# One weight tile in three of the last matrix product: its lower part by an accumulating DMA

## The chip, the cores and the metric

One core of one Trainium2 chip. The time is device time of one execution in microseconds (us), and lower is better.

## The reference

A decoder layer on x, 256 tokens by 2048 channels, in float32:

```python
h = rms_norm(x, norm1_g); z = h @ w_in                     # 2048 -> 13312
# ... three branches (pooling, Conformer convolution, gated short convolution), merged by sigmoid gates ...
x = x + merged @ w_o
h = rms_norm(x, norm2_g)
up = causal_dwconv(h @ ffn_up, ffn_conv_w)                 # 2048 -> 2 x 5504
gt, vl = jnp.split(up, 2, axis=-1)
x = x + (jax.nn.silu(gt) * vl) @ ffn_down                  # 5504 -> 2048: the product that is changed
out = rms_norm(x, final_g)
```

## The kernel before, in words

Every matrix product is made of three products of float32r operands. A weight tile w, loaded as float32 into `raw`, is split into an upper part `wh`, which is w rounded to float32r, and a lower part `wl` = w - wh. The activations are split in the same way and lie in one tile, upper part in the first 256 columns and lower part in the next 256. TensorE adds up act_high x wh, act_low x wh and act_high x wl in float32 in PSUM.

`load_w` (L67) makes one weight tile. SyncE (SP) issues the load of 128 x 1024 numbers, 512 KB, into a `raw` buffer (L64); ScalarE (ACT) copies it to `wh`, which rounds (L75); VectorE (DVE) subtracts `wh` from `raw` into `wl` (L76). There are five `raw` buffers and three each of `wh` and `wl` (L59, L72, L73). A tile's `wh` can be written when TensorE has made the last product with the `wh` that lay in the buffer before it; `wl` likewise; and the next load into a `raw` buffer can be issued when ACT and DVE have read it.

The last product, with `ffn_down`, is `gemm_n` (L128), called four times, once for each 512 output columns (L606 to L610). K is 5504, in 43 blocks of 128 rows; a weight tile holds two blocks (kt=2), so that one call has 22 tiles, the last of them a half. For each tile `products` issues eight matmuls with `wh` (L143 and L145 by turns) and then four with `wl` (L150), each of 512 columns. The first two tiles of the first call are made ahead, before the last posts of the stage before (L572). What follows a call (residual, squares, the norm's gain: `take`, L582) is a post; it is issued after the second tile of the next call (L158). The fourth call (L610) has its last eight blocks in a large buffer of their own and ends with `finish`.

The order of the instructions on each engine is fixed when the program is built, by a scheduler: it takes the instructions by priority (the order in which the code issues them) as their inputs and buffers come free by its own reckoning. On the chip each engine runs its queue in that order and waits at each instruction for the semaphores of what it depends on. GpSimd (POOL) has no DMA and no work in the calls of the last product but for one small power per half at the end (L598).

Of the kernel before, what the change touches and what calls it, by code (L numbers as in the profile page):

```python
# [12 lines left out]
F32 = mybir.dt.float32  # L13
F32R = mybir.dt.float32r
AF = mybir.ActivationFunctionType
ALU = mybir.AluOpType
PSUM = bass.MemoryType.PSUM

P = 128
# [6 lines left out]
KF = FF // P  # L26
# [17 lines left out]
def hybrid_block(ctx: ExitStack, tc, xT, x, vec, w_in, w_gate, gate_b, pool_w, pool_p, conf_p, sconv_p, w_o, up, down, fg, out):  # L44


    nc = tc.nc

    const = ctx.enter_context(tc.tile_pool(name="const", bufs=1))
    wp = ctx.enter_context(tc.tile_pool(name="wp", bufs=3))  # L50
# [7 lines left out]
    def load_raw(src):  # L58
        raw = wp.tile([P, 1024], F32, name="raw", bufs=5)  # L59
        n = math.prod(src.shape[1:])  # L60
        v = raw[:, 0:n]
        if len(src.shape) == 3:
            v = v.rearrange("p (a b) -> p a b", a=src.shape[1])
        held["load"] = nc.sync.dma_start(v, src).ins  # L64
        return v, n

    def load_w(src, dst=None):  # L67

        raw, n = load_raw(src)
        kt = src.shape[1]  # L70
        if dst is None:
            wh = wp.tile([P, 1024], F32R, name="wh")  # L72
            wl = wp.tile([P, 1024], F32R, name="wl")  # L73
            dst = [w[:, 0:n].rearrange("p (a b) -> p a b", a=kt) for w in (wh, wl)]
        nc.scalar.copy(dst[0], raw)  # L75
        held["split"] = nc.vector.tensor_sub(dst[1], raw, dst[0].bitcast(F32)).ins  # L76
        return dst

    posts = deque()
# [3 lines left out]
    def run_posts():  # L86
        while posts:
            posts.popleft()()
# [4 lines left out]
    def tick(n):  # L93

        due[0] += n
        while due[0] >= 1 and background:
            due[0] -= 1
            with tc.issue_after(held["split"]):
                background.popleft()()
        if not background:  # L100
            due[0] = 0
# [23 lines left out]
    def first_weights(src, n=2):  # L125
        return [load_w(src[:, 2 * i:2 * i + 2, :]) for i in range(n)]

    def gemm_n(src, act, nk, kt=2, ahead=(), ticks=0, last=None, finish=None):  # L128

        if last is None:
            ps = psg.tile([P, 2, 512], F32, name="g")
            out = [ps[:, t, :] for t in range(2)]
        else:
            out = [psm.tile([P, 512], F32, name="m") for t in range(2)]

        def products(ts, k0, wh, wl):
            n = wh.shape[1]
            for kk in range(n):  # L140
                k = k0 + kk
                for t in ts:
                    nc.tensor.matmul(out[t], lhsT=act[:, k, t * P:(t + 1) * P], rhs=wh[:, kk, :],  # L143
                                     start=(k == 0), stop=False)
                    nc.tensor.matmul(out[t], lhsT=act[:, k, S + t * P:S + (t + 1) * P], rhs=wh[:, kk, :],  # L145
                                     start=False, stop=False)
            for kk in range(n):
                k = k0 + kk
                for t in ts:
                    nc.tensor.matmul(out[t], lhsT=act[:, k, t * P:(t + 1) * P], rhs=wl[:, kk, :],  # L150
                                     start=False, stop=(k == nk - 1))

        nb = nk - (8 if last is not None else 0)
        for i, k0 in enumerate(range(0, nb, kt)):
            n = min(kt, nb - k0)
            products((0, 1), k0, *(ahead[i] if i < len(ahead) else load_w(src[:, k0:k0 + n, :])))
            tick(ticks)
            if i == 1:  # L158
                run_posts()
        if last is not None:  # L160
            chunks = [(k0, load_w(src[:, k0:k0 + 2, :], [last[:, o + k0 - nb:o + k0 - nb + 2, :] for o in (0, 8)]))
                      for k0 in range(nb, nk, 2)]
            for t in range(2):
                for k0, w in chunks:
                    products((t,), k0, *w)
                finish(t, out[t])
        return out
# [315 lines left out]
    def branch(b, n, proj, act, ticks=0, ahead=()):  # L483
        posts.append(gate(b, n, gemm_n(w_gate[4 * b + n], hT, KD, ticks=ticks, ahead=ahead)))
        posts.append(add_branch(b, n, gemm_n(proj[n], act, KW, ticks=ticks)))

    ahead = first_weights(w_gate[0])
# [3 lines left out]
    for n in range(4):  # L491
        branch(0, n, pool_p, bA, 2, ahead)
        ahead = ()
# [7 lines left out]
    ahead = first_weights(w_o[0])  # L501
# [9 lines left out]
    def residual(ps, xs, ss):  # L511

        nc.vector.tensor_add(xs, ps, xs)
        nc.scalar.activation(scratch, xs, AF.Square, accum_out=ss)
# [28 lines left out]
    for n in range(4):  # L543
        posts.append(norm_chunk(n, gemm_n(w_o[n], merged, KD, ahead=ahead)))
        ahead = ()
# [4 lines left out]
    fa = fpool.tile([P, KF, 2 * S], F32R, name="fa")  # L550
    background.extend([*pause(1), second_mean_squares, second_rstd])
    with tc.tile_pool(name="up", bufs=2) as upp:
# [19 lines left out]
        ahead = first_weights(down[0])  # L572
# [9 lines left out]
    def take(n, ps):  # L582
        def go():
            for t in range(2):
                residual(ps[t], x1[:, t, 512 * n:512 * n + 512], ss3[:, t, n:n + 1])
            xs = x1[:, :, 512 * n:512 * n + 512]
            nc.vector.tensor_mul(xs, xs, fgb[:, 512 * n:512 * n + 512].unsqueeze(1).broadcast_to([P, 2, 512]))
            if n == 2:
                nc.vector.reduce_sum(part, ss3[:, :, 0:3], axis=mybir.AxisListType.X)
                nc.vector.tensor_scalar(part, part, 1.0 / D, EPS, op0=ALU.mult, op1=ALU.add)  # L590
        return go

    def finish(t, ps):

        r = const.tile([P, 1], F32, name=f"r3{t}")
        residual(ps, x1[:, t, 1536:D], ss3[:, t, 3:4])
        nc.vector.tensor_scalar(r, ss3[:, t, 3:4], 1.0 / D, part[:, t:t + 1], op0=ALU.mult, op1=ALU.add)
        nc.gpsimd.tensor_tensor(r, r, neg_half[:, 0:1], op=ALU.pow)  # L598
        nc.scalar.activation(x1[:, t, 0:768], x1[:, t, 0:768], AF.Copy, scale=r)
        nc.scalar.dma_start(ov[:, t, 0:768], x1[:, t, 0:768])  # L600
        nc.vector.tensor_scalar_mul(x1[:, t, 768:1536], x1[:, t, 768:1536], r)
        nc.sync.dma_start(ov[:, t, 768:1536], x1[:, t, 768:1536])
        nc.vector.scalar_tensor_tensor(x1[:, t, 1536:D], x1[:, t, 1536:D], r, fgb[:, 1536:D], op0=ALU.mult, op1=ALU.mult)
        nc.sync.dma_start(ov[:, t, 1536:D], x1[:, t, 1536:D])

    for n in range(3):  # L606
        posts.append(take(n, gemm_n(down[n], fa, KF, ahead=ahead)))
        ahead = ()
    room = hp.tile([P, 16, 512], F32R, name="hT")
    gemm_n(down[3], fa, KF, last=room, finish=finish)  # L610
# [48 lines left out]
```

## Time and profile before

| | |
|---|---|
| median of 2 runs | 1500.69 us (1499.91 to 1501.47) |
| the profiled execution's own time | 1499.96 us |
| its span, first to last instruction | 1498.2 us |
| TensorE (PE) busy | 1480.2 us, 99% |
| DVE busy | 1051.6 us, 70% |
| ACT busy | 733.3 us, 49% |
| POOL busy | 22.8 us, 2% |
| mean granted TensorE clock | 0.998 of full speed |

The span runs from the first instruction to the last; the execution's own time has some 1.8 us around it. Busy shares are means over the whole program. The calls of the last product begin at about 1255.8 us of the span and their products end at about 1489.9 us.

### The profile page before, as it was taken

To read this page: it belongs to the slowest core of one execution; us is meant where nothing else is said; L and a number is where in the kernel's file an instruction comes from. 1 tells how busy PE (TensorE), PEld (TensorE's weight loads), DVE (VectorE), ACT (ScalarE), POOL (GpSimd) and SP (SyncE) were. 2 spreads that over 40 slices of the span, in tenths; PEclk is the share of its full clock that TensorE was granted. 3 is DMA by queue.
4 is the path that set the end of the run, shared out by engine and by line. 5 is a ranking of instruction groups with operands and counts; after the bars stand their busy time and mean duration, and the time that the engine had idled before them with its cause. 6 is when DMAs were issued, how large, how long until landed. Compare 5 with 4: busy or idle time off the path is not lost.

```text
span 1498.2 us, 19991 instructions
## 1 busy us (share of the span) xinstructions
PE 1480.2 (99%) x7546; PEld 1263.8 (84%) x7546; DVE 1051.6 (70%) x1402; ACT 733.3 (49%) x935; POOL 22.8 (2%) x87
## 2 busy tenths in 40 slices
PE   7999999999999999999999999999999999999997
PEld 6888888888888888888888888888888888888886
DVE  5868888888888775555557777777777777455453
ACT  6554454444444454444555555555555555344343
POOL 0000000000001100000000000000000000000000
PEclk9999999999999999999999999999999999999999
DMA  8755555676666666667655555555555556666663
GB/s 274 241 190 189 176 190 185 183 233 202 198 207 198 199 201 197 193 193 239 185 184 188 188 188 190 188 189 189 189 189 187 191 186 217 192 199 194 188 199 120
DMA packets 83169, 293.13 MB, mean 196 GB/s; under 512 B 9344, under 2 KB 9856, under 8 KB 82688
## 3 DMA queue, kind: packets, MB, share of 16 engines
q1 hardware_dynamic: 82640, 291.06, 61.3%
q8 instruction: 59, 0.97, 0.2%
q10 hardware_dynamic: 432, 0.79, 0.1%
q14 instruction: 38, 0.31, 0.1%
HBM read 289.72 MB, written 2.10 MB: 195 GB/s over the span
## 4 chain that ended last, share of the span: by engine, by line
PE 97%; DMA 2%; issue 0%; DVE 0%; ACT 0%; DVEq 0%; POOLq 0%; POOL 0%; SPq 0%; ACTq 0%
PE g L114 32%; PE g L118 17%; PE g L143 15%; PE g L145 15%; PE g L150 15%; DMA raw<-in_w_in 1%; PE m L150 1%; PE m L143 1%; PE m L145 1%; DMA raw<-in_xT 0%; PE m L478 0%; PE m L527 0%; ACT wh L75 0%; DVE wl L76 0%; DMA g<-in_vec 0%
## 5 line engine op out<-in xcount | busy, mean ns | idle before, releaser
L76 DVE TENSOR_TENSOR wl<-raw,wh 128x1024 fp32r<-128x1024 f32 (+1 forms) x537 | 650.1, 1212 | 372.0 <-ACT wh L75 365.9
L75 ACT CAST wh<-raw 128x1024 fp32r<-128x1024 f32 (+1 forms) x537 | 556.4, 1036 | 651.3 <-PE g L145 265.5
L114 PE MATMUL g<-hT,wh 128*128 128x512 f32 x2144 | 539.9, 393 | 9.7 <-ACT wh L75 5.3
L114 PEld LDWEIGHTS g<-hT,wh 128*128 128x128 f32 x2144 | 385.5, 189 | 80.0 <-ACT wh L75 11.4
L118 PEld LDWEIGHTS g<-hT,wl 128*128 128x128 f32 x2144 | 293.7, 191 | 21.7
L118 PE MATMUL g<-hT,wl 128*128 128x256 f32 x2144 | 300.1, 282 | 0.0
L143 PE MATMUL g<-wh,hT 128*128 128x512 f32 x384 | 150.1, 391 | 0.0
L145 PE MATMUL g<-wh,hT 128*128 128x512 f32 x384 | 149.5, 389 | 0.0
L284 DVE SCALAR_TENSOR_TENSOR confwork<-confwork,vecs 128x256 f32<-128x256 f32 x240 | 106.3, 478 | 0.0
L150 PE MATMUL g<-wl,hT 128*128 128x512 f32 x384 | 102.7, 389 | 0.0
L145 PE MATMUL g<-wh,fa 128*128 128x512 f32 x258 | 100.4, 389 | 0.0
L143 PE MATMUL g<-wh,fa 128*128 128x512 f32 x258 | 100.4, 389 | 0.0
L150 PEld LDWEIGHTS g<-wl,hT 128*128 128x128 f32 x384 | 72.1, 188 | 15.0
L145 PEld LDWEIGHTS g<-wh,hT 128*128 128x128 f32 x384 | 72.1, 188 | 14.8
L143 PEld LDWEIGHTS g<-wh,hT 128*128 128x128 f32 x384 | 72.1, 188 | 14.8
L563 DVE SCALAR_TENSOR_TENSOR cv<-sp,vecs,cv 128x256 f32<-128x256 f32 x172 | 71.7, 479 | 0.0
L150 PE MATMUL g<-wl,fa 128*128 128x512 f32 x258 | 69.2, 389 | 0.0
L150 PEld LDWEIGHTS g<-wl,fa 128*128 128x128 f32 x258 | 48.4, 188 | 10.1
L143 PEld LDWEIGHTS g<-wh,fa 128*128 128x128 f32 x258 | 48.4, 188 | 10.0
L145 PEld LDWEIGHTS g<-wh,fa 128*128 128x128 f32 x258 | 48.4, 188 | 10.0
L143 PE MATMUL g<-wh,merged 128*128 128x512 f32 x128 | 50.1, 391 | 0.0
L145 PE MATMUL g<-wh,merged 128*128 128x512 f32 x128 | 49.8, 389 | 0.0
(145 smaller groups left out, 1079.5 us busy)
## 6 DMA issues: line engine op xcount, KB each, us to landing
raw<-in_up SPq DMA_DIRECT2D x172, 512.0 KB, 4.6
raw<-in_w_gate SPq DMA_DIRECT2D x96, 512.0 KB, 4.4
raw<-in_w_in SPq DMA_DIRECT2D x92, 512.0 KB, 4.3
raw<-in_down SPq DMA_DIRECT2D x84, 512.0 KB, 4.2
raw<-in_w_o SPq DMA_DIRECT2D x32, 512.0 KB, 3.6
raw<-in_pool_p SPq DMA_DIRECT2D x16, 512.0 KB, 5.0
raw<-in_sconv_p SPq DMA_DIRECT2D x16, 512.0 KB, 4.7
raw<-in_conf_p SPq DMA_DIRECT2D x16, 512.0 KB, 4.5
```

Source lines behind the costliest of these rows:

```text
L75: nc.scalar.copy(dst[0], raw)
L76: held["split"] = nc.vector.tensor_sub(dst[1], raw, dst[0].bitcast(F32)).ins
L114: nc.tensor.matmul(ps[:, j, :], lhsT=wh[:, kk, j * P:(j + 1) * P], rhs=act[:, k0 + kk, :], start=(k0 + kk == 0), stop=False)
L118: nc.tensor.matmul(ps[:, j, 0:S], lhsT=wl[:, kk, j * P:(j + 1) * P], rhs=act[:, k0 + kk, 0:S], start=False, stop=(k0 + kk == nk - 1))
L143: nc.tensor.matmul(out[t], lhsT=act[:, k, t * P:(t + 1) * P], rhs=wh[:, kk, :], start=(k == 0), stop=False)
L145: nc.tensor.matmul(out[t], lhsT=act[:, k, S + t * P:S + (t + 1) * P], rhs=wh[:, kk, :], start=False, stop=False)
L150: nc.tensor.matmul(out[t], lhsT=act[:, k, t * P:(t + 1) * P], rhs=wl[:, kk, :], start=False, stop=(k == nk - 1))
L284: nc.vector.scalar_tensor_tensor(acc[:, c, :], src, w, acc[:, c, :], op0=ALU.mult, op1=ALU.add)
L563: nc.vector.scalar_tensor_tensor(cv[:, h, :], sp[:, h, q:q + S], V("ffn_w", c + q), cv[:, h, :], op0=ALU.mult, op1=ALU.add)
```

## The change

A second loader, `load_w_dma`, and a flag `by_dma` of `gemm_n`. In the first three calls of the last product the tiles with i % 3 == 2 (i = 2, 5, 8, 11, 14, 17, 20, seven in each call) are made by it. ACT writes `wh` as before, then a second time over the same size: `wl` = -wh. Then POOL issues a DMA from `raw` to `wl` that adds what it brings to what lies there, so that `wl` = w - wh. DVE has no part in these tiles. All other tiles, and the fourth call, are as before.

```diff
+    def load_w_dma(src):
+        raw, n = load_raw(src)
+        wh, wl = (wp.tile([P, 1024], F32R, name=w)[:, 0:n].rearrange("p (a b) -> p a b", a=src.shape[1]) for w in ("wh", "wl"))
+        nc.scalar.copy(wh, raw)
+        nc.scalar.activation(wl, wh.bitcast(F32), AF.Copy, scale=-1.0)
+        nc.gpsimd.dma_start(wl, raw, accum_op=ALU.add)
+        return wh, wl
...
-    def gemm_n(src, act, nk, kt=2, ahead=(), ticks=0, last=None, finish=None):
+    def gemm_n(src, act, nk, kt=2, ahead=(), ticks=0, last=None, finish=None, by_dma=False):
...
-            products((0, 1), k0, *(ahead[i] if i < len(ahead) else load_w(src[:, k0:k0 + n, :])))
+            load = load_w_dma if by_dma and i % 3 == 2 else load_w
+            products((0, 1), k0, *(ahead[i] if i < len(ahead) else load(src[:, k0:k0 + n, :])))
...
-        posts.append(take(n, gemm_n(down[n], fa, KF, ahead=ahead)))
+        posts.append(take(n, gemm_n(down[n], fa, KF, ahead=ahead, by_dma=True)))
```

## Rows read from the trace of the kernel before

**Rows 1.** The page's part 4, the chain of work that ended last, by engine.
```profile
PE 97%; DMA 2%; issue 0%; DVE 0%; ACT 0%; DVEq 0%; POOLq 0%; POOL 0%; SPq 0%; ACTq 0%
```

**Rows 2.** Waits of TensorE in the whole span: total us, times, longest us.
```profile
PE g L114 <- ACT wh L75: 5.3, 8, 1.0
PE g L114 <- DVE hT L254: 4.4, 1, 4.4
```

**Rows 3.** Busy time by stretch, two calls of the last product: columns in the first line.
```profile
core 0: us, PE busy (x) PEld busy (x) DVE busy (x) ACT busy (x) POOL busy (x), PEclk, DMA share, GB/s
...
1316.00:1375.00 59.00, 59.00 (x262) 48.87 (x261) 29.13 (x26) 24.64 (x27) 0.00 (x0) 1.00 0.66 194
1375.00:1434.00 59.00, 59.00 (x262) 48.83 (x262) 29.13 (x27) 24.64 (x29) 0.00 (x0) 1.00 0.65 195
```

**Rows 4.** Waits of all engines from 1300 to 1430 us.
```profile
ACT wh L75 <- PE g L145: 77.2, 47, 2.1
DVE wl L76 <- ACT wh L75: 63.6, 42, 2.2
```

**Rows 5.** Timeline in order of time: start, duration, engine, line, operation.
```profile
1340.61 1.07 PE L150 MATMUL g<-wl,fa 128*128 128x512 f32 x4
...
1343.33 1.07 PE L150 MATMUL g<-wl,fa 128*128 128x512 f32 x4
1343.52 1.05 ACT L75 CAST wh<-raw 128x1024 fp32r<-128x1024 f32 x1 [1.67 <-PE g L145]
...
1344.61 1.22 DVE L76 TENSOR_TENSOR wl<-raw,wh 128x1024 fp32r<-128x1024 f32 x1 [1.50 <-ACT wh L75]
...
1346.05 1.07 PE L150 MATMUL g<-wl,fa 128*128 128x512 f32 x4
...
1348.77 1.07 PE L150 MATMUL g<-wl,fa 128*128 128x512 f32 x4
```

**Rows 6.** DMA queues and issues from 1300 to 1430 us: count, size, us to landing.
```profile
q1 hardware_dynamic: 7043, 25.12, 65.4%
...
raw<-in_down SPq DMA_DIRECT2D x47, 512.0 KB, 3.6
raw<-in_down SPq DMA_DIRECT2D x2, 256.0 KB, 2.8
```

**Rows 7.** POOL's groups in the whole span: busy us, mean ns of one.
```profile
L556 POOL MEMSET sp<- 128x4 f32 x43 | 4.3, 102 | 626.6 <-DVE cv L563 435.1 <-PE m L478 168.8 <-ACT cv L565 22.7
L189 POOL TENSOR_TENSOR r<-r,neg_half 128x2 f32<-128x2 f32 x2 | 2.3, 1138 | 129.9 <-DVE r L188 129.9
L598 POOL TENSOR_TENSOR r<-r,neg_half 128x1 f32<-128x1 f32 x2 | 1.1, 550 | 251.5 <-DVE r L597 251.5
```

**Rows 8.** Timeline where the second call's half tile ends, about 1372 us.
```profile
1372.34 0.62 PE L150 MATMUL g<-wl,fa 128*128 128x512 f32 x2
1372.54 1.05 ACT L75 CAST wh<-raw 128x1024 fp32r<-128x1024 f32 x1 [0.76 <-PE g L145]
...
1373.72 0.64 ACT L514 ACTIVATE scratch<-x 128x512 f32<-128x512 f32 x1
```

**Rows 9.** Busy time by stretch at the end, PEclk the granted clock.
```profile
1485.00:1490.00 5.00, 4.91 (x22) 3.75 (x20) 1.75 (x5) 1.67 (x3) 0.55 (x1) 1.00 0.34 131
1490.00:1492.00 2.00, 0.00 (x0) 0.00 (x0) 0.86 (x2) 0.72 (x2) 0.28 (x1) 1.00 0.53 197
1492.00:1494.00 2.00, 0.00 (x0) 0.00 (x0) 1.28 (x2) 0.94 (x1) 0.28 (x1) 0.69 0.12 43
1494.00:1498.00 4.00, 0.00 (x0) 0.00 (x0) 0.00 (x0) 0.00 (x0) 0.00 (x0) 0.50 0.63 241
```

## The prediction, made before the changed kernel ran

> **What bounds the kernel now.** I read the chain of waits first: TensorE carries 97% of it [rows 1]. The next question is whether TensorE ever waits, so I took its own waits: 9.7 us in the whole span, in two groups on L114, a line that the last product does not run [rows 2]. The busy time by stretch agrees: in two calls of the last product TensorE is busy for 59.0 of 59 us at full granted clock, DVE for 29.1, ACT for 24.6, POOL for nothing, and the DMA engines are busy 0.65 to 0.66 of the time [rows 3]. So in the stage that is changed nothing but TensorE's own work sets the time.
>
> Who waits for whom there [rows 4]: ACT's cast waits for TensorE (47 times, 77 us), DVE's subtraction waits for ACT. That is the sign of engines that run as far ahead as the buffers let them, and the question of the change is how far that is.
>
> The timeline gives it [rows 5]. The four matmuls of a lower part begin at 1340.61, 1343.33, 1346.05 and 1348.77, so that a tile takes TensorE 2.72 us and three tiles 8.16. Call the begin at 1343.33 the point w. At w the upper buffer of that tile is free, ACT's cast of the tile three further on begins at w + 0.19 and lasts 1.05; DVE begins at w + 1.28, lasts 1.22 and is done at w + 2.50. That lower part is wanted at w + 8.16. It lies ready for 5.66 us before it is used.
>
> **The change, part by part.**
>
> *Removed:* 21 subtractions of 1.22 us on DVE, 25.6 us. DVE has some 30 of 59 us free in this stage and no engine's work in it waits for DVE in the waits read [rows 3, 4]. Worth nothing, and TensorE has no idle time in this stage from which a gain could come: the lower bound of the whole change is nought.
>
> *Added on ACT:* 21 more passes over 128 x 1024 numbers. I take the cast's 1.05 us for each [rows 5], 22 us in all. ACT is idle 1.67 us before each cast, and the second pass fits into it: cast from w + 0.19 to w + 1.24, negation from w + 1.28 to w + 2.33; the next cast begins at w + 2.91. The lower buffer is free by then (its last matmul ends at w + 1.07). Nothing is pushed; the cover is the idle time of ACT, and without it a cast would come up to 1.05 us late, which its own lead over TensorE, longer still, would take up. After a half tile two squares of a post stand close behind the cast [rows 8]; they come 1.05 us later and only a post waits for them.
>
> *Added on POOL and the DMA engines:* from w + 2.33 the accumulating DMA has until w + 8.16, that is **5.83 us** from the end of the negation until TensorE may read. Whatever it needs beyond this, TensorE waits, once per such tile: the buffers of `wl` are three and the changed tiles are every third, so that each of them takes the buffer of the one before it, and the wait cannot be worked off in between. After a half tile, which the first changed tile of the second and third call meets, two matmuls are missing and the time is 0.45 us shorter (0.62 against 1.07) [rows 8, 5].
>
> What the DMA needs no row shows: there is no DMA from POOL in this kernel, and none that adds. It reads the weight tile, reads what ACT has written, and writes the sum: 512 KB each. The nearest row is a load of the same 512 KB, 3.6 us from issue to landing in this stage. The queue's share gives what of that is occupation of the engines: 65.4% of 130 us for 48 tiles' worth (47 full and two halves) is 1.77 us for 512 KB [rows 6]. Bounds for the whole step:
> - low: a load's 3.6 plus POOL's shortest instruction, 0.10 [rows 7]: 3.7 us, inside the 5.83, cost nothing;
> - high: 3.6, plus 1.77 each for the second read and for a write that is not overlapped, plus two loads in front of it on the same engines at 1.77, plus POOL's longest small operation, 1.14 [rows 7]: 11.8 us, a wait of 6.0 and 126 us over 21 tiles.
>
> I take the middle by what surely is added to a load: one further read (1.77), one load beside it (1.77, since loads keep the engines busy two thirds of the time [rows 3] and come in a burst when a late `raw` buffer is given back), and 0.55 for POOL to take it up, its shorter two-operand instruction [rows 7]. 3.6 + 1.77 + 1.77 + 0.55 = 7.69 us; a wait of 1.86 us; 21 x 1.86 = 39.1, and twice 0.45 for the half tiles: **40 us**.
>
> Two rules on that step, apart from the sum. The Trainium skill, "Collectives: The Full Stack", section "The bandwidth ceiling: the fold count and why AG ≠ RS ≠ AR", says that an add in the DMA engines issues two reads per piece and so goes at half the rate of a copy; by that, the engines' 1.77 would be 3.54, as in the sum. The Trainium skill, "DMA: Bandwidth & Descriptors", section "Anatomy of one DMA — SWDGE (gpsimd) path", gives 2.0 us plus bytes over 436 GB/s for a DMA issued from GpSimd; as an estimate by that page 512 KB takes 3.2 us, there would be no wait, and the sum would be nought. No row here shows either.
>
> *Moved:* `raw` is given back when the DMA has landed, not at w + 2.50. SP's load for the tile five on waits for that, and every load behind it on SP's queue with it. With 7.69 us it comes free at w + 10.0; the load lands 3.6 later, w + 13.6, where its cast would have begun at w + 0.19 + 5 x 2.72 = w + 13.8. So the loads just hold; and a cast may come some 5 us late before TensorE needs it (three tiles, 8.16 us, less the 1.05 of the cast and 1.82 by which upper products come ahead of the lower). Cost nothing up to a DMA of about 13 us.
>
> The sum is made against the profiled execution, 1499.96 us (span 1498.2 and 1.8 around it): 1540. The median of the runs shown lies 0.73 above it, which gives **1541 us**.
>
> **The rivals.**
>
> *The DMA is hidden.* It needs no more than 5.83 us: for instance as a load, 3.6, and 0.55 for POOL, 4.15. For it: both its sources and its target are tiles on the core, the second read may be overlapped, and the budget leaves 1.7 us over this price. Against: two reads, the loads beside it, a kind of issue that no row shows. Point from which it decides: 5.83 us. Time: no change, 1500 to 1502. The Trainium skill's rule of 2.0 us plus bytes over 436 GB/s would give this same case. Chance 0.27.
>
> *Late by less than 1.4 us each*, a DMA between 5.83 and 7.2 us: up to 30 us, 1503 to 1530; a part of my mechanism that still counts as no change at 2% (about 30 us, which is what a measurement of this kernel can tell from none). Chance 0.13.
>
> *The DMA engines become the bound.* If an accumulating tile occupies them for three crossings (5.3 us), three tiles ask 3 x 1.77 + 5.3 = 10.6 us of 8.16, 2.5 us over, 7 times in each call: 51 us, inside my forecast's range; with latencies in series as well it is the high bound, 1627. There TensorE's clock comes in: after its last matmul at about 1490 us the granted clock is 1.00 for the first 2 us, 0.69 in the next two, 0.50 after that [rows 9], so waits of about 2 us leave the full level (2.4 GHz), and much longer ones lead to the lower (1.2 GHz), where a tile's 2.72 us would double: up to 57 us more for 21 tiles. Chance 0.11 for over 1600.
>
> *Faster*: would need TensorE's matmuls themselves to shorten; they run back to back, twelve in 2.72 us [rows 5], and nothing of the change touches them. Chance 0.02. That the scheduler puts the negation behind another cast, or a lower part elsewhere, would only move w + 2.33 later and belongs to the late cases.
>
> **How the numbers follow.** Forecast (late by 1.4 to 4.7 us each, 1530 to 1600): 0.47. With the heavy case slower by over 2% has 0.58; the hidden and the slightly late ones give 0.40 within; faster 0.02. The range reaches from the hidden case, 1499, to 1600, a DMA of some 10.5 us; left out are the heavy case and the little below. The forecast's own range is 1530 to 1600.
>
> **What would show it.** In the changed profile: TensorE waits on L150 (or on its weight loads) for a DMA into `wl`, 21 times, near 1.9 us each, and three changed tiles' period near 10 us instead of 8.16; DMA share above 0.65 in the first three calls; DVE busy about 20 us in a call instead of 29, ACT about 32 instead of 25; the fourth call unchanged. I am wrong if TensorE has no idle time there (the landing of POOL's DMA is then below 5.8 us), if the waits sit on the casts or on L64 (then it is `raw`), or if the granted clock falls.

## The result, and the profile after

The changed kernel takes 1509.88 us in the median (1509.34 and 1510.43) against 1500.69: a ratio of 1.0065, interval 1.0049 to 1.0081. It is slower by 9.2 us, clear of noise and far below 2%. The sign was forecast, the size was not: 40 us were forecast. The profiled execution has 1510.43 us and a span of 1508.6.

First TensorE's waits, the view of [rows 2], from 1250 to 1450 us of the changed kernel (total us, times, longest us):

```profile
PE g L159 <- DMA wl<-raw: 6.4, 3, 3.5
```

L159 is L150 of before: the products with the lower part. It waits for the accumulating DMA as forecast, but at 3 of the 21 changed tiles, not at all of them. Where they stand, by the timeline (start, duration, then in brackets the idle time before):

```profile
1276.00 1.26 PE L159 MATMUL g<-wl,fa 128*128 128x512 f32 x4 [3.54 <-DMA wl<-raw]
...
1319.05 1.19 PE L159 MATMUL g<-wl,fa 128*128 128x512 f32 x4 [0.34 <-DMA wl<-raw]
...
1364.08 1.20 PE L159 MATMUL g<-wl,fa 128*128 128x512 f32 x4 [2.57 <-DMA wl<-raw]
```

Begin to begin, three such steps take 6.42, 3.22 and 5.46 us where the tile period is 2.72: 3.7, 0.5 and 2.7 us. The first also costs clock. The busy time by stretch around it (PEclk is the granted clock):

```profile
1262.00:1272.00 10.00, 10.00 (x46) 8.23 (x45) 5.02 (x7) 5.48 (x7) 0.88 (x1) 1.00 0.97 292
1272.00:1276.00 4.00, 0.47 (x4) 0.04 (x2) 0.10 (x1) 1.04 (x1) 0.00 (x0) 1.00 0.84 235
1276.00:1281.00 5.00, 5.00 (x15) 3.99 (x16) 0.00 (x0) 1.41 (x2) 0.87 (x1) 0.66 0.84 250
```

After 3.5 us in which TensorE stood still the clock granted is 0.66 in the mean of 5 us, and the next lower part begins 4.44 us later (at 1280.44), not 2.72: 1.7 us more. Sum: 3.7 + 1.7 + 0.5 + 2.7 = 8.6 us. The span is 10.4 longer; about 1.0 us of that lay ahead of the first changed tile already (the first lower products of the last product begin at 1258.67, not 1257.64), and the other 0.8 us are small differences between the waits and after the last matmul.

A usual changed tile, the counterpart of [rows 5], in the timeline:

```profile
1302.23 1.07 PE L159 MATMUL g<-wl,fa 128*128 128x512 f32 x4
1302.47 1.05 ACT L83 CAST wh<-raw 128x1024 fp32r<-128x1024 f32 x1 [1.71 <-PE g L154]
1303.56 1.06 ACT L84 ACTIVATE wl<-wh 128x1024 fp32r<-128x1024 f32 x1
1304.92 0.87 POOL L85 DMA_DIRECT2D wl<-raw  x1 [7.29 <-ACT wl L84]
...
1310.39 0.84 PE L159 MATMUL g<-wl,fa 128*128 128x512 f32 x3
```

With w = 1302.23 the negation ends at w + 2.39 and POOL starts 0.30 us later. The lower part is wanted at w + 8.16, 5.5 us after POOL's start. And the DMA needs, by the line of its 21 issues (us from issue to landing):

```profile
DMA to landing us min/median/max: 4.7/4.9/8.9
```

So the usual one has 0.6 us to spare: 5.5 less 4.9. DMA queues and issues from 1300 to 1430 us, the view of [rows 6]:

```profile
q1 hardware_dynamic: 6789, 23.94, 54.3%
q0 software_dynamic: 2211, 8.01, 34.8%
...
raw<-in_down SPq DMA_DIRECT2D x44, 512.0 KB, 4.1
wl<-raw POOLq DMA_DIRECT2D x15, 512.0 KB, 4.8
```

q0 is POOL's queue: 34.8% of 130 us for 8.01 MB is 2.96 us of all 16 engines for one 512 KB tile; the loads take 1.55 (54.3% for 45.5 tiles). The engines are 0.89 busy instead of 0.65. The rest is as forecast: in the undisturbed third call DVE is busy 20.2 of 59 us (29.1 before) and ACT 31.5 (24.6) [rows 3].

```profile
1375.00:1434.00 59.00, 59.00 (x262) 48.84 (x261) 20.16 (x18) 31.51 (x34) 6.53 (x8) 1.00 0.92 256
```

### The profile page after: what moved, and what is told of

Its sections match the earlier page's. It is cut to its first block, busy times and chain, and to the rows that moved or that the text cites. A ratio compares the mean times of both kernels' runs of the same rounds, so it can differ in the third digit from the quotient of the medians.

```text
span 1508.6 us, 20052 instructions
## 1 busy us (share of the span) xinstructions
PE 1482.9 (98%) x7546; PEld 1264.8 (84%) x7546; DVE 1025.8 (68%) x1381; ACT 754.7 (50%) x956; POOL 41.3 (3%) x108
## 4 chain that ended last, share of the span: by engine, by line
PE 94%; DMA 3%; ACT 1%; issue 1%; DVE 0%; SPq 0%; DVEq 0%; POOLq 0%; POOL 0%; ACTq 0%
PE g L123 32%; PE g L127 16%; PE g L159 14%; PE g L152 14%; PE g L154 14%; DMA wl<-raw 2%; DMA raw<-in_w_in 1%; PE m L152 1%; PE m L159 1%; PE m L154 1%; DMA raw<-in_xT 0%; PE m L488 0%; PE m L537 0%; ACT wh L75 0%; ACT wl L84 0%
## 5 line engine op out<-in xcount | busy, mean ns | idle before, releaser
L76 DVE TENSOR_TENSOR wl<-raw,wh 128x1024 fp32r<-128x1024 f32 (+1 forms) x516 | 624.4, 1211 | 405.8 <-ACT wh L75 389.6
L75 ACT CAST wh<-raw 128x1024 fp32r<-128x1024 f32 (+1 forms) x516 | 534.2, 1035 | 599.6 <-PE g L154 216.9
L159 PE MATMUL g<-wl,hT 128*128 128x512 f32 x384 | 102.7, 389 | 0.0
L159 PEld LDWEIGHTS g<-wl,hT 128*128 128x128 f32 x384 | 72.1, 188 | 15.0
L159 PE MATMUL g<-wl,fa 128*128 128x512 f32 x258 | 69.7, 391 | 6.4 <-DMA wl<-raw 6.4
L159 PEld LDWEIGHTS g<-wl,fa 128*128 128x128 f32 x258 | 48.3, 188 | 17.7 <-DMA wl<-raw 7.7
```

## The experiments

All ratios are to the kernel before, run on the same chip between the others.

**The changed kernel again.** No edit.

> The changed kernel once more, nothing edited. Theory A (margin): an accumulating DMA lands 4.9 us after POOL takes it up, 0.6 us inside the time it has, and only single late ones cost; the late one beside the load of the final gain row (1 MB, issued at 1265 us of the span) has a cause in the program and comes again with 3 to 4 us of wait, the other two (0.7 and 3 us) hang on single DMA engines that fall behind and move to other tiles or go. Median 1505 to 1511. Theory B (general load): every changed tile costs a little, and the three waits of the profile stand for that; then the same three waits come at the same places.

1509.65 us (1507.75 to 1511.13), ratio 1.0063 [1.0048, 1.0078]. Its profile has two waits:

```profile
1275.90 2.08 PE L159 MATMUL g<-wl,fa 128*128 128x512 f32 x4 [4.53 <-DMA wl<-raw]
...
1363.09 1.20 PE L159 MATMUL g<-wl,fa 128*128 128x512 f32 x4 [2.51 <-DMA wl<-raw]
```

The first came again. So did the third, at the same tile, which theory A had not said; the second went. In this profile the clock fell behind the shorter wait too, and the next lower part began 4.40 us after it:

```profile
1363.00:1368.00 5.00, 4.91 (x14) 3.91 (x15) 0.00 (x0) 1.32 (x2) 0.87 (x1) 0.66 0.69 198
```

Before it, in the profile shown first, TensorE had waited 2.57 us at this tile and kept a granted clock of 1.00; here it waited 2.51 and got 0.66. So the length of a wait does not settle whether the clock falls.

**The gain row's load elsewhere.** The 1 MB load of `fgb` (L589 in the changed kernel) is issued at 1265.22 us; POOL's second DMA starts at 1267.03 and lands 8.9 us later. By the packets of the trace (pieces of at most 4 KB) its first one starts 4.1 us after POOL does; at 19 of the other 20 changed tiles that is 1.4 to 1.5 us, at the first 1.6. So most of its delay lies ahead of its first packet.

```diff
+    fgb = xp.tile([P, D], F32, name="fgb")          # beside scratch, ahead of the second norm
+    nc.sync.dma_start(fgb, fg.broadcast_to([P, D]))
...
-    fgb = fin.tile([P, D], F32, name="fgb")
-    nc.sync.dma_start(fgb, fg.broadcast_to([P, D]))
```

> The changed kernel with the load of the final gain row moved from the start of the last product to before the second norm, so that no 1 MB load runs beside the second accumulating DMA. Theory A: the wait of 3.5 us at the second changed tile and the 2.3 us that its lowered clock costs go, median 5 to 6.5 us below the changed kernel, 1503 to 1505. Theory B: no change, 1509.

1502.28 us (1500.51 to 1506.65), ratio 1.0019 [1.0008, 1.0029]: 7.4 us below the run of the changed kernel beside it, more than the 5 to 6.5 expected. TensorE has no wait in the last product in this profile, and the slowest landing is 5.7 us:

```profile
DMA to landing us min/median/max: 4.7/4.8/5.7
```

Theory B falls: 21 changed tiles are still there, and three quarters of the loss are gone. Not all of the 7.4 us is accounted for: the wait at the second changed tile and the slower clock after it cost 5.4 us in the first profile and 6.2 in the second. The later wait is missing too in the profile of this run, and nothing in the edit shows why.

**The control for it**: the same edit in the kernel before.

> The kernel before, with nothing but the gain row's load moved as in the run with the early gain row: the control for that run. Theory A: the load costs nothing in the kernel before, so 1499 to 1501, no difference. Rival: the early place gains by itself, 1496 to 1498, and then the run with the early gain row hides a loss of that size.

1500.31 us, ratio 1.0000 [0.9990, 1.0009]. The place of that load is worth nothing by itself; it matters only where an accumulating DMA runs beside it.

**Four lower buffers.**

```diff
-            wl = wp.tile([P, 1024], F32R, name="wl")
+            wl = wp.tile([P, 1024], F32R, name="wl", bufs=4)
```

(and likewise in the new loader)

> The changed kernel with four buffers for the lower part in place of three, so that each has one tile more, 2.72 us, before it is wanted: 8.5 us in place of 5.8. Theory A: all waits but at most 0.7 us at the gain row's load go, median 1501 to 1503. Theory B: if the cost is not the wait for the lower part but the load on the DMA engines, 1507 to 1510.

1509.39 us, ratio 1.0064 [1.0049, 1.0079]; waits of 4.20 and 2.52 us. This looks like theory B, but it was my edit that failed. In its timeline the cast of a changed tile still begins 0.24 us after the lower products of the tile three before:

```profile
1301.96 1.07 PE L159 MATMUL g<-wl,fa 128*128 128x512 f32 x4
1302.20 1.05 ACT L83 CAST wh<-raw 128x1024 fp32r<-128x1024 f32 x1 [1.71 <-PE g L154]
```

What starts the chain is the upper buffer, of which there were still three. The run gave the DMA no time and tells nothing of the theories.

**Four of both.** `bufs=4` for `wh` and `wl`, in both loaders.

> The changed kernel with four buffers for the upper part as well as for the lower, since with four for the lower alone the cast and the negation behind it still began when the third upper buffer came free. Now the chain begins a whole tile, 2.72 us, earlier: 8.5 us in place of 5.8. Theory A (margin): the waits of 2.5 us in the second call go, the one beside the gain row's load falls from 3.5 to 4.5 us to 0.8 to 1.8, and TensorE's clock stays full; median 1501 to 1504. Theory B (the load on the DMA engines itself costs): 1507 to 1510.

1502.28 us (1500.70 to 1507.29), ratio 1.0015 [1.0005, 1.0024], with the gain row's load where the change has it. The longest of three waits in the profile (the others are 0.33 and 0.42 us):

```profile
1272.50 1.20 PE L159 MATMUL g<-wl,fa 128*128 128x512 f32 x4 [0.87 <-DMA wl<-raw]
```

And the landing of its 21 accumulating DMAs:

```profile
DMA to landing us min/median/max: 4.7/6.5/9.0
```

A tile's period more of lead leaves 1.8 us over the kernel before in place of 9.6, about as much gained as by moving the load: the loss is the wait for late DMAs and not the work that they put on the engines. The engines are as busy as in the changed kernel (0.87 to 0.90 against 0.88 to 0.91 in the same stretches), and yet the usual DMA, begun earlier, lands after 6.5 us and not 4.9; by the packets its first one comes 1.4 to 4.8 us after POOL's start. So 4.9 us is not a fixed price at this load of the engines: when the DMA begins decides it too.

**Half a microsecond of margin, tried from the other side.**

```diff
         nc.scalar.activation(wl, wh.bitcast(F32), AF.Copy, scale=-1.0)
+        nc.scalar.activation(wl, wh.bitcast(F32), AF.Copy, scale=-1.0)
```

> The changed kernel with ACT's negation written twice, so that each accumulating DMA begins 1.06 us later, with all else alike. Theory A (margin of 0.6 us at each changed tile): each of 21 is now late by some 0.45 us, so 9 to 12 us over the changed kernel, median 1518 to 1523, with waits at nearly every changed tile. Rival: the usual tile has far more room than the landing times say and only the late ones grow, 1511 to 1513.

1521.62 us, ratio 1.0146 [1.0131, 1.0161]: 21.2 us over the kernel before, where the changed kernel had 9.6 on its chip; 11.5 more, 0.55 for each of 21 tiles. Here L86 is the DMA and L160 the lower products; of 21 changed tiles the profile shows TensorE's weight loads waiting at 20 and its matmuls at 13 (who waited for the DMA: us, times):

```profile
  PEld g L160: 20.8, 20
  PE g L160: 11.4, 13
```

The landing is 4.9 us as before. So the margin was as small as read: 1.06 us later, and the usual tile is late by half of that.

**Without the add.**

```diff
-        nc.gpsimd.dma_start(wl, raw, accum_op=ALU.add)
+        nc.gpsimd.dma_start(wl, raw)
```

> The changed kernel with the DMA only copying the weight over the lower part, not adding (so the lower part holds the whole weight; this leaves the subtraction out). It separates the price of the add from that of a DMA issued by POOL. Theory A with two reads per add: the DMA engines' time falls from 2.96 to 1.6 us per tile, landing from 4.9 to 3.5 us, no waits but perhaps beside the gain row, median 1501 to 1503. Rival: POOL's issue makes the time and the add is free: landing stays above 4.5 us, median 1506 to 1510.

1506.77 us, ratio 1.0045 [1.0028, 1.0062]. Its queues and issues from 1300 to 1430 us:

```profile
q0 software_dynamic: 2160, 7.87, 16.6%
...
wl<-raw POOLq DMA_DIRECT2D x16, 512.0 KB, 3.0
```

A plain copy of the same tile by POOL lands in 3.0 us and takes the engines 1.44 us (16.6% for 15 tiles); the add costs 1.8 and 1.5 us more. The rival (an add that is free) falls. But my time was wrong: I expected 1501 to 1503. One wait stays, 3.12 us at the second changed tile, beside the gain row, where the copy lands after 8.5 us, and the clock granted in the 5 us after it is 0.66. So that late landing is not made by the add.

**Two of three tiles.**

```diff
-            load = load_w_dma if by_dma and i % 3 == 2 else load_w
+            load = load_w_dma if by_dma and i % 3 != 0 and i >= 2 else load_w
```

> The changed kernel with two of three tiles made by the accumulating DMA (14 of 22 in each call). The DMA engines are then asked for 3 x 1.55 + 2 x 2.96 = 10.6 us of work per three tiles, which take TensorE 8.16. Theory A with the engines' capacity: 2.4 us lost per three tiles, 51 us over 21 such groups, median 1545 to 1570. Rival (only the time of one DMA against its own margin counts): 1510 to 1520.

1547.51 us, ratio 1.0318 [1.0303, 1.0333]. The edit makes 13 tiles of a call in this way, not 14, since it leaves out i = 1: 39 DMAs, 18 groups of three with two of them and three groups with one. TensorE waits 17 times, 33.5 us. The rival falls, and the size is that of the engines' capacity: by this run's queues from 1300 to 1430 us an accumulating tile occupies the engines for 2.68 us and a load for 1.59, so that three tiles with two such DMAs ask 3 x 1.59 + 2 x 2.68 = 10.1 us. From 1358.69 to 1398.92 four groups take 40.2 us, 10.1 each, and the engines are busy 0.97 around it:

```profile
1360.00:1420.00 60.00, 51.25 (x221) 40.77 (x220) 11.61 (x11) 32.31 (x34) 9.59 (x11) 1.00 0.97 257
```

The DMAs land after 7.4 us in the median. A rival is left: POOL also waits for an earlier accumulating DMA to land before it issues the next, 12 times, 72.9 us in all. The run does not separate this order from the share of the engines.

The clock fell here after waits as short as 2.09 us; the granted clock from 1326.4 to 1331.4 us is 0.66:

```profile
1326.36 1.85 PE L159 MATMUL g<-wl,fa 128*128 128x512 f32 x4 [2.09 <-DMA wl<-raw]
```

**The wait in the second call.** In the packets of the trace it belongs to one DMA engine. (The packets carry no engine's number; here one is followed by each packet beginning where the one before it ends.) Of the DMA that starts at 1355.87, 15 engines are done by 1360.4 and one at 1363.7. That one moves 16 packets of loads, one behind the other, until 1360.56, and only then its eight of the accumulating DMA, the first five without a gap (start in us, queue, ns):

```
1360.408 q1 159
1360.564 q1 9     (the load's last, 4 bytes)
1360.569 q0 327
1360.876 q0 328
1361.185 q0 328
1361.493 q0 328
1361.801 q0 328
1362.109 q1 173
1362.279 q0 327
...
1363.708 q0 9     (the last, 4 bytes)
```

At the two accumulating DMAs before, the last engine was 0.15 and 0.34 us late; that it was the same one is likely and not shown. I suspected the fetch of 16 KB of instructions that occupies one engine for 0.95 us at 1340.6, just ahead of the tenth accumulating DMA, and took that tile out.

```diff
-            load = load_w_dma if by_dma and i % 3 == 2 else load_w
+            load = load_w_dma if by_dma and i % 3 == 2 and (by_dma, i) != (2, 8) else load_w
...
-        posts.append(take(n, gemm_n(down[n], fa, KF, ahead=ahead, by_dma=True)))
+        posts.append(take(n, gemm_n(down[n], fa, KF, ahead=ahead, by_dma=n + 1)))
```

> The changed kernel with one of its 21 tiles, the third of the second call (i = 8), made by DVE again. In three profiles a 16 KB instruction fetch on one DMA engine stood 0.3 to 0.4 us ahead of that tile's accumulating DMA, that engine ended it late, was 0.3 to 0.5 us late at the next and 3.4 us at the one after, where TensorE waited 2.5 us. Theory (a late engine is not given time to catch up because of the accumulating DMAs): no such wait in the second call in the profile, the gain row's wait as before, median 1506 to 1508. Rival (the engine is late for another reason): the wait of about 2.5 us comes again in the second call, median 1508.5 to 1511.

1508.35 us (1507.50 to 1513.72), ratio 1.0050 [1.0034, 1.0065]: between the two expectations. The wait in the second call is gone, and one of the same kind, 2.91 us, has come in the third, at 1399.65. There one engine is 0.36 us late at one accumulating DMA and 3.7 us at the next. The last fetch of 16 KB lies 14 us ahead of the first of these; one of 8 KB, 0.31 us long, lies 2.3 us ahead. So a 16 KB fetch beside the DMA isn't needed, and this run doesn't tell what makes the engine late. The order in the expectation is not that of every profile either: with four lower buffers the 16 KB fetch stands only 0.1 us ahead, and the large lag comes at the next DMA already. And this profile is that of the slowest of four executions, 1513.72 us; the other three took 1507.50 to 1508.42, so it doesn't show what the median is made of.

**Every sixth tile, and the gain row early.**

```diff
-            load = load_w_dma if by_dma and i % 3 == 2 else load_w
+            load = load_w_dma if by_dma and i % 6 == 2 else load_w
```

(on top of the kernel with the early gain row)

> The kernel with the early gain row and every sixth tile in place of every third (i = 2, 8, 14, 20, four in each call). The DMA engines are busy 0.85 of the time in place of 0.93. Theory (late engines that cannot catch up make the 2 us that are left): nothing is left, 1500 to 1501, ratio to the kernel before 0.999 to 1.001, and no run above 1503. Rival (a cost of each changed tile): 12 of 21 tiles, 1501.3.

1501.00 us (1499.56 to 1502.22), ratio 1.0003 [0.9995, 1.0012]: no difference that can be measured, no run above 1503, no wait in the profile, and the engines busy 0.80. This agrees with late engines that matter at 0.89 to 0.92 busy and not at 0.80, but does not show it: with 12 DMAs in place of 21 there are also fewer that can be late. Of the rival, 1501.3, it says too little: that lies inside the interval.

## Why the prediction was right and wrong

**Right.** TensorE bounds the stage, and 25.6 us less on DVE are worth nothing. ACT's second pass hides in its idle time (no post, no cast and no load became a wait of TensorE). The chain upper buffer, cast, negation, DMA and the 5.83 us that it leaves were right to 0.1 us; the doubled negation showed that the point where it turns lies where it was put. `raw` is given back late (SP waits 21 times, 49.4 us, for the new DMA) and this reaches nobody: no cast waits for a load.

**Wrong: the step from the DMA's time to "a wait of 1.86 us", by the size of its terms, above all "one load beside it (1.77)".** I put the DMA at 7.69 us and so a wait at each of 21 tiles. Measured, from the negation's end: 0.30 until POOL starts, and 4.9 to landing, 5.2 in all. By terms:

| term | forecast | measured | from |
|---|---|---|---|
| a transfer of 512 KB and POOL's issue | 3.6 + 0.55 | 0.3 + 3.0 | plain copy by POOL |
| second read | 1.77 | 1.8 | landing with the add less without |
| a load beside it | 1.77 | 0 | usual tile: occupied for 2.96 us of engine time |

The terms measured add up to 5.1, to 5.2 with the median landing of all 21. The second read was nearly exact in the landing; of the engines' time the add costs 1.5 us. The load beside it, which I added because the engines are two thirds busy on average, is not there for the usual tile: a DMA's packets take 2.96 us of each engine, and from its first packet to its last it lasts 3.0 us, to within 0.05, in 10 of 21 cases (and at most 3.4 in another seven), so nothing comes between; nor does a load hold up its first packet, which starts 1.4 to 1.5 us after POOL. With four of both buffers the usual DMA does land 1.6 us later, so the term is not wrong everywhere; here the DMA begins where it meets no load. Some 2.5 us too much, 1.77 of it this term and the rest the transfer and POOL's issue, turned a margin of 0.6 us into a wait of 1.86 at every tile.

**Missed: what is late once.** The same term was left out where it does occur. The gain row, 1 MB in one load, stood in the profile of before among the DMA issues (us to landing last), at 1264.24 us of the span, 2 us ahead of where the second accumulating DMA was to begin, and I did not ask of the one-off transfers which of them would meet a DMA with a margin:

```profile
fgb<-in_fg SPq DMA_DIRECT2D x1, 1024.0 KB, 7.1
```

Moving it takes off 7.4 of the 9.6 us; 5.4 to 6.2 of them are seen in the two profiles of the changed kernel, a wait of 3.5 to 4.5 us and the clock after it. Of the clock I said that waits of about 2 us keep it and much longer ones don't. After the longer ones it fell in each profile looked at (3.54 us of wait, and 0.66 after it). But the shorter ones went either way: 2.57 us kept 1.00, while 2.51 in the next profile and 2.09 with two of three tiles were followed by 0.66. A wait of this length can so cost some 1.7 us more than itself, which my sum did not have; a granted clock that falls was one of the signs that I had named for being wrong.

**The rivals.** The hidden DMA, given 0.27, is what happened at 18 of 21 tiles; the case "late by less than 1.4 us each" names the size of the total but not its form. The engines' capacity as the bound has the right size at two tiles of three; at one of three, the change itself, it did not set the time.

The two rules on the DMA's price: the Trainium skill, "Collectives: The Full Stack", section "The bandwidth ceiling: the fold count and why AG ≠ RS ≠ AR", says of the reduction in a collective that its add goes at half the rate of a copy because of two reads. The rate agrees: a 4 KB packet takes 338 ns in the median with the add and 176 without; the reads themselves no trace here shows. The Trainium skill, "DMA: Bandwidth & Descriptors", section "Anatomy of one DMA — SWDGE (gpsimd) path", gives 3.2 us for 512 KB as an estimate by its fit. The plain copy's 3.0 agrees, the add's 4.9 does not.

**Open:** why one DMA engine falls behind by more than 3 us in some profiles (both of the changed kernel, that with four lower buffers, that with one tile left out), and why a lag of 0.3 us becomes 3.4 at the next. That it did its two loads first and the accumulating DMA after them is seen; what made it late is not. Open too is what makes the 2.3 us that are left in the median where the gain row is out of the way. In the one profile of that run, 2.5 us slower than the kernel before, no such wait stands: its lower products run for 232.1 us from the first to the last against 231.7 before, and 1.7 us of the difference lie ahead of the last product.

## What to carry to other kernels

For a DMA put into a pipeline, work out the time that the buffers leave it and compare it with two things: its usual duration, and the worst transfer that can meet it. Here the usual one fits with 0.6 us and costs no wait, and one 1 MB load that had been free costs 5 to 7 us. More load on the engines alone did not decide it: with a tile's period more of lead the same DMAs cost 1.8 us. More buffers help only if the buffer that starts the chain is among them.

## What the runs showed of the hardware

- An accumulating DMA of 512 KB between two tiles on the core: 4.9 us from POOL's start to landing, 2.96 us of all 16 engines, 0.87 us of POOL; the same without the add 3.0, 1.44 and 0.54.
- When the DMA begins counts: at 0.87 to 0.91 of the engines busy the median landing was 4.9 us in the change and 6.5 with four of both buffers; beside a 1 MB load the one DMA of the change landed after 8.9.
- On one engine that was behind, the packets of two queues did not alternate at first: 16 packets of loads, then five of the accumulating DMA, then by turns.
- After 3.5 us without matmuls the granted clock was 0.66 in the mean of the next 5 us. After 2.57 us it stayed 1.00 in one execution; after 2.51 in another and 2.09 in a third it was 0.66.
